# The last projection of a two-layer trunk: tiles 4 to 7 by Strassen's scheme

## The chip, the cores and the metric

The kernel runs on one core of a Trainium2 chip. The metric is the device time of one execution in microseconds. A core has five engines that run side by side, each with its own in-order queue of instructions: TensorE (PE; PEld is its loading of weights), VectorE (DVE), ScalarE (ACT), GpSimd (POOL) and SyncE (SP, which here only issues transfers; ScalarE's queue issues some as well). They meet through semaphores. TensorE writes to eight banks of PSUM, from which VectorE and ScalarE read.

## What is computed

Two layers, each with one mixer of three head groups, on 1024 tokens of 1024 values in float32:

```python
def hybrid_layer(x, c_act, positions, ...):
    mod = c_act @ w_mod + b_mod
    shift, scale, gate = jnp.split(mod[:, None, :], 3, axis=-1)
    h = rms_norm(x, pre_gain) * (1.0 + scale) + shift
    proj = h @ w_in
    ...   # a_out: windowed attention; r_out: retention; g_out: gated linear attention, each times its gate
    y = jnp.concatenate([a_out, r_out, g_out], axis=-1) @ w_out
    return x + gate * rms_norm(y, post_gain)
```

The change concerns `y = concat(...) @ w_out` and the line after it, in the second layer only, and there the second half of the tokens.

## The kernel before

**Tiles.** The 1024 tokens are eight tiles of 128 (`NT`), in four pairs (`NP_`); the 1024 inner values are eight slices of 128 (`KT`, index k). A float32 product is made from two parts of each operand in the faster matmul type fp32r: a high part (a rounded copy) and a low part (the rest). `PASSES` takes high x high, low x high and high x low, so that 128 tokens by 512 columns by all 1024 inner values are 3 x 8 = 24 matmuls into one PSUM bank (`accum`).

**Weights** lie in seven places of two arenas (`PLACES`), high and low part side by side. In the last layer, the output weights `o0` to `o3` (256 columns each) stand in places 3 to 6; places 0 and 1 hold the normalised input of tiles 4 to 7, and place 2 the last gate weights, all of them used for the last time by the gate products just ahead of the output projection. `unit(l, name)` gives a place; `both(x, y)` joins two slices of 256 columns into one operand of 512.

**The mixed tiles.** The output of the heads goes to DRAM as `mixS[t]`: for every tile the high and the low part, 8 slices of 128x128 each, transposed. Slices 4 to 7 (retention, linear attention) come from `head_norm_gate` through `store_mix`; slices 0 to 3 (attention) from `gate`, for four tiles at a time. The last `gate` stores end just after 903 us of the profile. `load_mix(l, t)` brings a tile back in two transfers of 512 KB into one of two `mx` buffers (tile 7, by `MIXP`, into an arena place that is free by then).

**The output stage.** For each tile, two calls of `y_half` (one for each 512 columns) run 24 matmuls each, then ScalarE squares the bank and sums (line 1247) and VectorE multiplies it by the gate (1248). `finish` works out the row's factor (lines 534, 528, and a power on GpSimd, 529), loads the residual `xs`, adds (1292) and stores to `out`. For the last layer's tiles 6 and 7 the first halves run before the second halves. The last half of tile 7 is `y_last`: two pieces of 256 columns, so that less is left to do behind the last matmul (lines 1257 to 1266).

**Order.** TensorE's instructions run in the order in which the program emits them. That order comes from a clock that the program keeps while it is built (`clk`): every matmul adds its cost, `flag(name, lat)` says when a result will be there (the latencies are in the table `L`), `await_flag` moves the clock on, and work that waits for something is a generator given to `job`, which `pump` continues when its time has come. The instructions of the other engines and of the transfer queues are put in order by the tile framework, by when their inputs and buffers are ready in its own model; on the chip each queue then runs strictly in that order. Buffers are rings by tag: `t2` (12 of 128x512), `t1` (8 of 128x256), `st` (11, used for raw weights), `smx` (6, used by the softmax), `va` (8), `kT0` and `kT1` (one each, keys), `mx` (2), and PSUM in `mm` (5 banks) and `aux` (3). `EN` gives the engine of each small operation.

Of the kernel before, what the change touches and what calls it, by code (L numbers as in the profile page):

```python
# [10 lines left out]
F32 = mybir.dt.float32  # L11
# [6 lines left out]
P = 128  # L18
# [71 lines left out]
def trunk(ctx: ExitStack, tc: tile.TileContext, ins, cst, out):  # L90
# [161 lines left out]
    xs = dr.tile([NT, P, D], F32, name="xs")  # L252
    mixS = dr.tile([NT, P, 2, KT, P], F32, name="mixS")
# [996 lines left out]
    def y_last(l, mixt, ss, yg):  # L1250
        s3 = small(3)
        for u in range(2):
            pm = mm()[:, 0:256]
            w = unit(l, f"o{2 + u}")
            accum(pm, lambda a, k: mixt[:, a, k, :], lambda b, k: w[:, b, k, 0:256])
            c = slice(256 * u, 256 * u + 256)
            A.activation(yg[:, c], pm, AF.Square, accum_out=s3[:, u:u + 1])
            if u == 0:
                V.tensor_tensor(s3[:, 2:3], ss[:, 0:1], s3[:, 0:1], ALU.add)
                V.tensor_scalar(s3[:, 2:3], s3[:, 2:3], 1.0 / D, EPS, ALU.mult, ALU.add)  # L1260
                V.tensor_tensor(yg[:, c], pm, modg[l][:, 512 + 256 * u:768 + 256 * u], ALU.mult)
        r = small(1)
        q = V.scalar_tensor_tensor(r, s3[:, 1:2], 1.0 / D, s3[:, 2:3], ALU.mult, ALU.add)
        G.tensor_tensor(r, r, mhalf[:, 0:1], ALU.pow)
        with tc.issue_after(q.ins):
            V.tensor_tensor(yg[:, c], pm, modg[l][:, 768:1024], ALU.mult)
        return r

    def load_mix(l, t):
# [6 lines left out]
        if l == DEPTH - 1 and t in MIXP:  # L1276
            n, o, _ = PLACES[TOK[l][t // 2]]
            o += t % 2 * 2 * KT * P
            mixt = arenas[n][:, o:o + 2 * KT * P].rearrange("p (a k n) -> p a k n", a=2, k=KT)
        else:  # L1280
            mixt = mix_tile()
# [4 lines left out]
    def finish(l, t, ss, yg, r=None):  # L1286
        r = rstd2(ss) if r is None else r
        xt = [t2(), t2()]
        for j in range(2):
            sl = slice(512 * j, 512 * j + 512)  # L1290
            dma("lx", xt[j], x_in[0, t * P:(t + 1) * P, sl] if l == 0 else xs[t, :, sl])
            V.scalar_tensor_tensor(xt[j], yg[j], r, xt[j], ALU.mult, ALU.add)  # L1292
            dma("sx", out[0, t * P:(t + 1) * P, sl] if l == DEPTH - 1 else xs[t, :, sl], xt[j])
# [19 lines left out]
    def layer(l):  # L1313
# [121 lines left out]
        def gate(g, hf, kk, pm):  # L1435
# [9 lines left out]
            V.scalar_tensor_tensor(ao, th, 0.5, ao, ALU.mult, ALU.mult)  # L1445
            mh, ml = t2(F32R), t2(F32R)
# [13 lines left out]
        for hf in range(2):  # L1460
# [8 lines left out]
            if not hf:  # L1469
                load(l, "o0")  # L1470
                load(l, "o1")
        mx[0] = load_mix(l, 0)
# [17 lines left out]
        for t in range(NT - 2, NT):  # L1490
            r = None
            if t == NT - 1:
                r = y_last(l, hold[t][0], hold[t][1], hold[t][2][1])
            else:
                y_half(l, t, 1, hold[t][0], hold[t][1], hold[t][2][1])
            job(finish(l, t, hold[t][1], hold[t][2], r))
# [67 lines left out]
```

## Time and profile before

| | us |
|---|---|
| median of 3 runs | 971.76 (971.18 to 973.42) |
| profiled execution, its own time | 971.16 |
| its span in the profile | 969.4 |
| TensorE busy | 951.3 (98%) |
| VectorE busy | 640.2 (66%) |
| ScalarE busy | 410.1 (42%) |
| GpSimd busy | 272.5 (28%) |
| granted TensorE clock, mean | 0.996 |

How to read the lines that follow. A row of the timeline has the start, the length (both us), the engine, the line of the program, the operation, output<-inputs by name, and, in brackets, how long the engine had been idle and what ended that. A row of a group has the line, engine, operation and shapes, the count, then the busy time in us and the mean of one in ns, then the idle time of the engine just before and what ended it. A row of the stage table has, for a stretch of time, the busy time and the number of instructions of PE, PEld, DVE, ACT and POOL, then the granted clock, the mean busy share of the sixteen transfer engines and the GB/s they moved. Much of the program goes through small helpers: line 161 is every matmul, 150 every transfer of `dma`, 145 every ScalarE copy. Matmuls are pipelined, so a row's single length is more than the time from one matmul to the next.

### The profile page before, as it was taken

The page shows a single profiled execution, that of the slowest core. Times are in us where ns is not written, and L with a number is a line of the kernel's source. Part 1 is how long each engine was busy: PE and PEld are TensorE (multiplying, and loading weights), DVE is VectorE, ACT ScalarE, POOL GpSimd, SP SyncE. Part 2 cuts the span into 40 slices and gives each one's busy share as a digit, 9 for nine tenths or more (in the row PEclk, how much of TensorE's full clock was granted, in tenths as well). Part 3 has the DMA queues.
Part 4 walks back from the last instruction along what each step waited for, and adds up shares of the span by engine and source line. Part 5 has one row for each costly group of instructions (what it writes and reads, how often), then busy time and mean ns, then how long its engine had stood idle before and what let it go on. Part 6 is the DMA issues. An engine that isn't in the chain of part 4 may idle for free.

```text
span 969.4 us, 18061 instructions
## 1 busy us (share of the span) xinstructions
PE 951.3 (98%) x6513; PEld 829.4 (86%) x6513; DVE 640.2 (66%) x1525; ACT 410.1 (42%) x1119; POOL 272.5 (28%) x323
## 2 busy tenths in 40 slices
PE   6999999999999999999999999999999999999997
PEld 1799999989998877878889999998999887777886
DVE  6886857777777777655586485686776577763332
ACT  2777312354422666622455531134652166761111
POOL 3243011533430344511242110144423034441000
PEclk9999999999999999999999999999999999999999
DMA  9943314624335355677455160253222333555871
GB/s 313 320 146 110 111 56 129 187 77 112 115 102 150 98 168 180 218 242 237 172 166 172 50 180 22 83 155 92 80 86 77 120 88 105 158 174 174 261 238 65
DMA packets 124293, 140.30 MB, mean 145 GB/s; under 512 B 12734, under 2 KB 95528, under 8 KB 124204
## 3 DMA queue, kind: packets, MB, share of 16 engines
q1 hardware_dynamic: 116204, 127.43, 42.9%
q10 hardware_dynamic: 8000, 11.72, 3.4%
q8 instruction: 51, 0.84, 0.4%
q14 instruction: 38, 0.31, 0.1%
HBM read 102.42 MB, written 34.60 MB: 141 GB/s over the span
## 4 chain that ended last, share of the span: by engine, by line
PE 86%; DMA 7%; DVE 3%; issue 2%; POOL 1%; ACT 0%; SPq 0%; DVEq 0%; ACTq 0%; POOLq 0%
PE mm L161 67%; PE aux L161 15%; PE aux L176 4%; DMA wm<-in_w_mod_dram 2%; DMA t<-in_x_dram 1%; DMA st<-in_w_in_dram 1%; DMA xk<-in_x_dram 1%; DMA t<-aoS 1%; DMA st<-in_w_mod_dram 1%; POOL sm L529 1%; DVE acc L367 0%; DVE t L1292 0%; POOL arena L491 0%; DVE t L624 0%; DMA c_ident<-cst_ident_dram 0%
## 5 line engine op out<-in xcount | busy, mean ns | idle before, releaser
L161 PE MATMUL mm<-arena,arena 128*128 128x256 f32 (+2 forms) x1896 | 303.0, 315 | 1.4 <-ACT arena L628 0.7
L161 PE MATMUL mm<-arena 128*128 128x256 f32 (+2 forms) x1824 | 294.7, 317 | 0.0
L161 PEld LDWEIGHTS mm<-arena,arena 128*128 128x128 f32 x1896 | 261.8, 188 | 24.6 <-ACT arena L628 1.2
L161 PEld LDWEIGHTS mm<-arena 128*128 128x128 f32 x1824 | 255.4, 191 | 22.0 <-issue 1.2
L161 PE MATMUL mm<-arena,mx 128*128 128x512 f32 (+1 forms) x744 | 168.7, 386 | 0.0
L161 PEld LDWEIGHTS mm<-arena,mx 128*128 128x128 f32 x744 | 135.6, 188 | 29.1 <-issue 1.5
L529 POOL TENSOR_TENSOR sm<-sm,mhalf 128x4 f32<-128x4 f32 (+1 forms) x60 | 51.8, 863 | 294.8 <-DVE sm L528 285.3
L491 POOL TENSOR_TENSOR arena<-st,arena 128x512 fp32r<-128x512 f32 x55 | 80.3, 1467 | 91.3 <-ACT arena L145 34.7
L145 ACT ACTIVATE t<-aux 128x512 f32<-128x512 f32 (+1 forms) x96 | 48.7, 521 | 106.4 <-PE aux L176 44.9
L943 POOL TENSOR_TENSOR smx<-smx,sm 128x512 f32<-128x512 f32 x32 | 36.2, 1131 | 114.8 <-DVE sm L942 111.4
L491 DVE TENSOR_TENSOR arena<-st,arena 128x512 fp32r<-128x512 f32 x65 | 62.3, 969 | 4.7 <-PE mm L161 2.6
L145 ACT ACTIVATE arena<-st 128x512 fp32r<-128x512 f32 x82 | 48.5, 626 | 29.0 <-PE mm L161 13.0
L1247 ACT ACTIVATE t<-mm 128x512 f32<-128x512 f32 x30 | 17.9, 597 | 92.2 <-PE mm L161 40.3
L939 ACT ACTIVATE smx<-smx,sm 128x129 f32<-128x129 f32 x128 | 50.0, 393 | 14.0 <-DVE sm L936 13.9
L1248 DVE TENSOR_TENSOR t<-mm,modg 128x512 f32<-128x512 f32 x30 | 20.6, 689 | 48.6 <-ACT t L1247 48.5
L367 DVE SCALAR_TENSOR_TENSOR acc<-st,c_act,acc 128x512 f32<-128x512 f32 x60 | 47.3, 788 | 7.5 <-DMA st<-in_w_mod_dram 6.8
L1292 DVE SCALAR_TENSOR_TENSOR t<-t,sm,t 128x512 f32<-128x512 f32 x32 | 25.9, 846 | 39.7 <-DMA t<-xs 20.8
L176 PE MATMUL aux<-c_ident,t 128*128 128x128 f32 x288 | 45.5, 278 | 2.9 <-DVE t L602 2.9
L176 PEld LDWEIGHTS aux<-c_ident,t 128*128 128x128 f32 x288 | 34.9, 144 | 7.3 <-DVE t L602 4.2
L934 DVE COPY_PREDICATED smx<-c_curmask,aux 128x256 f32<-128x256 int32 x64 | 25.5, 447 | 15.0 <-ACT smx L145 10.4
L990 ACT ACTIVATE t<-aux 128x256 f32<-128x256 f32 x32 | 12.2, 382 | 54.1 <-PE aux L161 26.8
L995 DVE TENSOR_TENSOR t<-aux,sm 128x256 f32<-128x256 f32 x32 | 13.6, 425 | 30.8 <-POOL sm L529 30.8
(214 smaller groups left out, 1300.9 us busy)
## 6 DMA issues: line engine op xcount, KB each, us to landing
st<-in_w_in_dram SPq DMA_DIRECT2D x96, 256.0 KB
st<-in_w_mod_dram SPq DMA_DIRECT2D x64, 256.0 KB
mx<-mixS SPq DMA_DIRECT2D x30, 512.0 KB
mixS<-t SPq DMA_DIRECT2D x64, 128.0 KB
st<-in_w_out_dram SPq DMA_DIRECT2D x32, 256.0 KB
mixS<-t SPq DMA_DIRECT2D x32, 256.0 KB
wm<-in_w_mod_dram SPq DMA_DIRECT2D x12, 512.0 KB
t<-in_x_dram SPq DMA_DIRECT2D x24, 256.0 KB
```

The source lines that it names most:

```text
L145: A.activation(dst, src, AF.Copy)
L161: T.matmul(dst, lhsT, rhs, start=start, stop=stop)
L176: T.transpose(dst, src, idn)
L367: V.scalar_tensor_tensor(acc, wt, c_act[:, k:k + 1], acc, ALU.mult, ALU.add)
L491: i = (G if first == 0 and kc in LOG else V if first == 0 else eng(f"wlo{kc}")).tensor_tensor(wt[:, 1, 2 * kc:2 * kc + 2, 0:256], st, f(hi ...
L529: after[2] = G.tensor_tensor(r, r, mhalf[:, :w], ALU.pow)
L934: V.copy_predicated(sv, curmask.unsqueeze(1).to_broadcast((P, 2, P)), pv[:, :, n // P - 1, :])
L939: A.activation(sm[:, h, :], sm[:, h, :], AF.Exp, bias=mx[:, h:h + 1], accum_out=sums[:, h:h + 1])
L943: eng("pn").tensor_tensor(sm[:, :, 0:128], sm[:, :, 0:128], rs.unsqueeze(2).to_broadcast((P, 4, P)), ALU.mult)
L1247: A.activation(yg, pm, AF.Square, accum_out=ss[:, nh:nh + 1])
L1248: V.tensor_tensor(yg, pm, modg[l][:, 512 * nh:512 * nh + 512], ALU.mult)
L1292: V.scalar_tensor_tensor(xt[j], yg[j], r, xt[j], ALU.mult, ALU.add)
```

## The change

In the second layer, tiles 0 to 3 are projected as before. Tiles 4 to 7 are taken in two pairs (p = 2 and 3). Of a pair, the two tiles, the two halves of the inner dimension (slices 0 to 3 and 4 to 7) and the two halves of the columns make 2x2 blocks A11 to A22 (tile, inner half) and B11 to B22 (inner half, column half). In place of eight block products, seven are made (Winograd's form of Strassen's scheme), each of 12 matmuls:

| m | A operand | B operand |
|---|---|---|
| 1 | A11 | B11 |
| 2 | A12 | B21 |
| 5 | A21 + A22 | B12 - B11 |
| 6 | A21 + A22 - A11 | B22 - B12 + B11 |
| 7 | A11 - A21 | B22 - B12 |
| 4 | A22 | B21 - (B22 - B12 + B11) |
| 3 | A12 - (A21 + A22 - A11) | B22 |

The four output blocks are then sums of products: 1+2; 1+6+7+4; 1+6+7+5; 1+6+5+3.

`load_sums` loads the 1024x1024 output weights a second time (sixteen pieces of 128x512), forms the B sums on VectorE and splits them into high and low part: blocks 5, 6, 7 into places 0, 1, 2, block 4 over the place of B12 after tile 3's product. The sums use the `smx` buffers and four `t2` buffers. For the A sums, the mixed tiles 4 to 7 are now also stored in full precision (`mixW`, by `head_norm_gate` and `gate`); `operands` loads four 256 KB halves of a pair, forms the four sums on VectorE and splits them. Unsummed blocks still come from `mixS`: the pair's first tile whole, of its second only slices 4 to 7, in eight pieces into `va` buffers. `outputs` lists the order of products, forms the output sums on VectorE (a ScalarE copy for product 1), squares and multiplies them from SBUF, and gives `finish` the tile. The last product (3 of pair 3, `tail`) is made in two pieces of 256 columns. In `finish`, the store of the last layer's output is now given out 1.5 us of the program's clock after the addition.

```diff
@@ head_norm_gate
         store_mix(t, kt0, pt[:, 0:256].rearrange("p (k q) -> p k q", k=2), 2)
+        if l == DEPTH - 1 and t >= 2 * NCL:
+            w = t1()
+            copy("mw", w, pt[:, 0:256])
+            dma("smw", mixW[t, :, kt0:kt0 + 2, :], w.rearrange("p (k q) -> p k q", k=2))
@@ gate
+            if l == DEPTH - 1 and hf * 4 + 3 >= 2 * NCL:
+                dma("smw", rows(mixW, hf, k), ao.rearrange("p (t q) -> p t q", t=4))
@@ load_sums (new)
+        for k in range(4):
+            raw = [gp.tile([P, 4, 129], F32, tag="smx", ...)[:, :, 0:P] for _ in range(3)]
+            hold.append(t2())
+            for r, (row, col) in zip(raw + [wide(hold[k])], ((0, 0), (0, 1), (1, 1), (1, 0))):
+                kt = 4 * row + k
+                dma("lwb", r, w_out[l, kt * P:(kt + 1) * P, 512 * col:512 * col + 512]...)
+            yield lat("bl2" if k else "bl1", l)
+            b11, b12, b22 = raw
+            if k > 1:
+                A.activation(b22, b22, AF.Copy, scale=gncol[:, l:l + 1])
+                A.activation(hold[k], hold[k], AF.Copy, scale=gncol[:, l:l + 1])
+            eng("ws5").tensor_tensor(b11, b12, b11, ALU.subtract)
+            eng("ws7").tensor_tensor(b12, b22, b12, ALU.subtract)
+            eng("ws6").tensor_tensor(b22, b22, b11, ALU.subtract)
+            eng("ws4").tensor_tensor(wide(hold[k]), wide(hold[k]), b22, ALU.subtract)
+            split("wl5", 5, k, b11)
+            split("wl7", 7, k, b12)
+            split("wl6", 6, k, b22)
...
+        yield (0.0, "plain")
+        for k in range(4):
+            hi, lo = weights(l, 4, 0, k), weights(l, 4, 1, k)
+            A.activation(hi, halves(hold[k]), AF.Copy)
+            eng("wl4").tensor_tensor(lo, halves(hold[k]), f(hi), ALU.subtract)
+            yield lat("bl4", l)
@@ operands (new), total
+            eng(f"os{m}").tensor_tensor(dst, x, y, op)
+            A.activation(hi, dst, AF.Copy)
+            eng(f"ol{m}").tensor_tensor(lo, dst, f(hi), ALU.subtract)
@@ outputs (new), rules
+            def first_():
+                A.activation(q, B[1], AF.Copy)
+            def c11():
+                V.tensor_tensor(y11, B[2], q, ALU.add)
+                square(y11, s0[:, 0:1])
+                eng("cg").tensor_tensor(y11, y11, gate[0], ALU.mult)
+            def sixth():
+                V.tensor_tensor(u2, B[6], q, ALU.add)
+            def seventh():
+                V.tensor_tensor(e, B[7], u2, ALU.add)
+            def c21_():
+                V.tensor_tensor(q, B[4], e, ALU.add)
+                square(q, s1[:, 0:1])
+                eng("cg").tensor_tensor(q, q, gate[0], ALU.mult)
+            def c22():
+                V.tensor_tensor(e, B[5], e, ALU.add)
+                V.tensor_tensor(u2, B[5], u2, ALU.add)
+                square(e, s1[:, 1:2])
+                eng("cg").tensor_tensor(e, e, gate[1], ALU.mult)
+                job(finish(l, 2 * p + 1, s1, [q, e]))
...
+            def tail():
+                for u in range(2):
+                    c = slice(256 * u, 256 * u + 256)
+                    b3 = mm()
+                    product(p, 3, b3, True, True, u)
+                    V.tensor_tensor(u2[:, c], b3[:, c], u2[:, c], ALU.add)
+                    i = square(u2[:, c], s0[:, 1 + u:2 + u])
+                    ...
@@ module level
-MIXP = (7,)
+FIN2 = 1
+NCL = 2
+MMP = (1, 2, 3, 4, 5, 6, 7)
+ORDER = [(2, "load"), (2, "half"), (2, 1), (2, 2), (3, "load"), (2, 5), (2, 6), (2, 7), (2, 4), (3, "half"), (2, 3), (3, 1), (3, 5), (3, 6), (3, 7), (3, 2), (3, 4), (3, "tail")]
```

More of the change, by code (lines that the diff above doesn't have):

```diff
@@ L1248, in y_half @@
         V.tensor_tensor(yg, pm, modg[l][:, 512 * nh:512 * nh + 512], ALU.mult)
[L1250 to L1267, printed above, removed]
@@ L1269, in load_mix, with block, weights, halves @@
-    def load_mix(l, t):
+    BLOCKS = {5: 0, 6: 1, 7: 2}
+    def block(m):
+        n, o, w = PLACES[BLOCKS[m]]
+        return arenas[n][:, o:o + 2 * KT * 256].rearrange("p (a k n) -> p a k n", a=2, k=4)
+    def weights(l, m, b, k):
+        if m in BLOCKS:
+            return block(m)[:, b, k]
+        u = 2 if m > 2 else 0
+        kt = k + (4 if m in (2, 3) else 0)
+        return both(unit(l, f"o{u}")[:, b, kt, 0:256], unit(l, f"o{u + 1}")[:, b, kt, 0:256])
+    def halves(ap):
+        return ap.rearrange("p (s n) -> p s n", s=2)
@@ L1270, in load_mix @@
+    def load_mix(l, t, half=False):
         if t < 2:
@@ L1275, in load_mix @@
             await_flag(("mix", l, t, kt0))
[L1276 to L1281, printed above, removed]
+        if half:
+            ts = [gp.tile([P, P], F32R, tag="va", name=nm("mh"), bufs=VDB) for _ in range(8)]
+            for i in range(8):
+                dma("lmix", f(ts[i]), mixS[t, :, i // 4, 4 + i % 4])
+            return ts
+        mixt = mix_tile()
         for a in range(2):
```

138 lines of the change are left out of this document (129 added, 9 removed).

## The prediction

> **What bounds the kernel now.** I read the page's engine rows first: is one engine the bound over the whole span, and at which clock?
>
> ```profile
> span 969.4 us, 18061 instructions
> PE 951.3 (98%) x6513; PEld 829.4 (86%) x6513; DVE 640.2 (66%) x1525; ACT 410.1 (42%) x1119; POOL 272.5 (28%) x323
> PEclk9999999999999999999999999999999999999999
> ```
>
> TensorE is busy for 98% at full clock, so work taken from it counts, if nothing then keeps it waiting. The change acts on the end of layer 1, so I next read its stretch of the chain that ended last (one line: start, us, what), and then the last microseconds of the timeline.
>
> ```profile
> 886.64 71.33 PE mm L161 x312
> ```
>
> ```profile
> 957.80 5.82 PE L161 MATMUL mm<-arena,arena 128*128 128x256 f32 x48
> ...
> 963.65 0.38 ACT L1257 ACTIVATE t<-mm 128x256 f32<-128x256 f32 x1 [2.29 <-DMA out_dram<-t]
> 963.93 0.19 ACT L1257 ACTIVATION_READ_ACCUMULATOR t<-mm 128x1 f32 x1
> 964.16 0.16 DVE L1263 SCALAR_TENSOR_TENSOR sm<-sm 128x1 f32<-128x1 f32 x1 [1.95 <-ACT t L1257]
> 964.24 0.42 DVE L1266 TENSOR_TENSOR t<-mm,modg 128x256 f32<-128x256 f32 x1
> 964.40 0.55 POOL L1264 TENSOR_TENSOR sm<-sm,mhalf 128x1 f32<-128x1 f32 x1 [4.10 <-DVE sm L1263]
> 964.98 1.42 DVE L1292 SCALAR_TENSOR_TENSOR t<-t,sm,t 128x512 f32<-128x512 f32 x2 [0.33 <-POOL sm L1264]
> ```
>
> From 886.64 on TensorE runs through without a break. The 312 matmuls are tiles 1 to 6 at 48 each and the first half of tile 7 (24): 71.33/312 = 0.2286 us for one 512 columns wide. The 48 of 256 columns that follow take 5.82/48 = 0.1213 us each. So tiles 4 to 7 begin at 886.64 + 3 x 48 x 0.2286 = 919.56 and their last matmul ends at 963.62. Behind it stand square, row factor, power and the last two multiply-adds (to 966.40), then the last transfer: 5.8 us to the span's end. Last, the stage table: what room have the engines that get the new work?
>
> ```profile
> core 0: us, PE busy (x) PEld busy (x) DVE busy (x) ACT busy (x) POOL busy (x), PEclk, DMA share, GB/s
> 860.00:880.00 20.00, 20.00 (x128) 15.31 (x127) 9.76 (x17) 9.56 (x31) 6.34 (x8) 1.00 0.59 185
> 880.00:900.00 20.00, 20.00 (x97) 15.80 (x96) 6.28 (x14) 2.64 (x9) 0.96 (x2) 1.00 0.55 180
> 900.00:920.00 20.00, 20.00 (x90) 16.32 (x89) 6.04 (x11) 2.09 (x7) 0.81 (x2) 1.00 0.91 292
> 920.00:940.00 20.00, 20.00 (x90) 16.56 (x89) 6.64 (x13) 2.62 (x8) 1.10 (x2) 1.00 0.76 257
> ```
>
> VectorE and ScalarE have two thirds free; the transfers have not, least of all between 900 and 920, just ahead of the tiles that are changed.
>
> **Part 1, the matmuls.** A pair had 2 tiles x 2 column halves x 2 halves of the inner dimension, eight blocks of 12 matmuls; now seven. Before, the two pairs took 963.62 - 919.56 = 44.06 us. After, 13 blocks of 12 at 0.2286 = 35.66 us and the last block in two halves, 24 at 0.1213 = 2.91 us: 38.57 us. Term: **-5.5 us**. The number of matmuls is fixed by the code, so that the change does not do this is no rival. By this clock pair 2 runs from 919.56 to 938.8, pair 3's sixth block ends at 955.2 and the last matmul at 958.1.
>
> **Part 2, the weight sums** (load_sums): sixteen loads of 256 KB; per k four sums and three low parts on VectorE, three high parts on ScalarE, and later the fourth block. The nearest rows, of the same shape:
>
> ```profile
> L1448 DVE TENSOR_TENSOR t<-t,t 128x512 fp32r<-128x512 f32 x4 | 3.1, 770 | 1.0 <-PE aux L161 0.9
> L1248 DVE TENSOR_TENSOR t<-mm,modg 128x512 f32<-128x512 f32 x15 | 10.3, 691 | 38.1 <-ACT t L1247 38.1
> L1292 DVE SCALAR_TENSOR_TENSOR t<-t,sm,t 128x512 f32<-128x512 f32 x16 | 11.3, 749 | 21.8 <-DMA t<-xs 20.8 <-POOL sm L529 0.7 <-POOL sm L1264 0.3
> L528 DVE TENSOR_SCALAR sm<-sm 128x1 f32<-128x1 f32 x7 | 1.1, 154 | 0.2
> L534 DVE TENSOR_TENSOR sm<-sm 128x1 f32<-128x1 f32 x7 | 1.1, 151 | 0.0
> L1247 ACT ACTIVATE t<-mm 128x512 f32<-128x512 f32 x15 | 9.0, 598 | 63.1 <-DVE t L1292 34.4 <-PE mm L161 28.7
> ```
>
> At 0.69 (the PSUM row; the row with both inputs in SBUF has 0.77) the 28 instructions ahead of the pairs are 19.3 us of VectorE, and 14 ScalarE copies at 0.60 are 8.4 us. The arena places that they write come free when the last gate product is done (about 870.5), and the first product with a summed block stands at 919.56 + 2 x 2.74 = 925.0. In those 54 us VectorE has about 19 us of old work by the table (half of the first row, two whole ones, a quarter of the last). Cost 0, covered by the plain tiles 0 to 3; if that cover is gone, the product of block 5 waits. The fourth block (four low parts, 2.8 us) is made after tile 3, since it overwrites weights that tile 3 reads, and is due at 933.3: 0. The four tiles that keep raw blocks leave eight of twelve t2 buffers for tiles 0 to 3, so their evictions may be late; ScalarE waited 34.4 us in five such waits (the L1247 row) and TensorE did not stall, with five banks to go on in. 0 again.
>
> **Part 3, the operand sums**: per pair four sums and four low parts on VectorE (8 x 0.69 = 5.5 us), four high parts on ScalarE (4 x 0.60 = 2.4 us). Pair 2's can begin once the last gates have stored their tiles, and are due one by one from 925.0 on. Counted with the output rules (11 VectorE passes of 512 a pair instead of 4), VectorE has between 919.56 and 955.2: rules 15 x 0.69 = 10.4, finishes of tiles 3 to 5 at 1.5 + 0.3 each = 5.4, tile 3's last product 0.7, pair 3's sums 5.5, the fourth block 2.8: 24.8 us of 35.6, and 30.3 (85%) if pair 2's sums also fall there. Under the bound: 0, with 0 to 3 us for the range.
>
> **Part 4, the transfers.** Added: 16 weight loads (4 MB), full-precision copies of the mixed tiles out (2 MB) and in (2 MB); 1 MB less of split tiles. SP gets some 48 more issues. What decides is the stretch ahead of 919.56:
>
> ```profile
> 904.00:906.00 2.00, 2.00 (x11) 1.65 (x10) 0.88 (x2) 0.65 (x2) 0.00 (x0) 1.00 1.07 354
> 936.00:938.00 2.00, 2.00 (x11) 1.65 (x10) 1.52 (x3) 0.69 (x2) 0.00 (x0) 1.00 1.01 397
> ```
>
> ```profile
> 907.88 2.76 SPq L150 DMA_DIRECT2D arena<-mixS  x2
> 910.69 0.90 SPq L150 DMA_DIRECT2D t<-xs  x2
> 911.69 1.16 SPq L150 DMA_DIRECT2D mx<-mixS  x2
> 917.46 1.41 DVE L1292 SCALAR_TENSOR_TENSOR t<-t,sm,t 128x512 f32<-128x512 f32 x2 [7.12 <-DMA t<-xs]
> ```
>
> Tile 4's split tile is issued at 911.69, when its buffer and the queue are free; the residual issued a microsecond before it was used only at 917.46, with VectorE waiting 7.12 us for it, so the queue was some 6 us deep. After the change tile 7's megabyte (907.88) is gone from this place, but both pairs' full-precision halves (2 MB), tile 5's halves (0.5 MB) and the last stores (0.5 MB) become ready just then, most of them before tile 4's buffer: 2 MB more. At 292/0.91 = 321 GB/s that is 6.2 us, of which the free 9% of the 20 us swallow 1.8: up to 4.4 us of lateness for the first product of pair 2. Ends 0 and 4.4; I take **+0.9**, near the low end, because that product needs only the first of tile 4's two transfers at first, and TensorE shows no wait of any size for a tile now. The block weights I put before 900, where these rows have room:
>
> ```profile
> 872.00:874.00 2.00, 2.00 (x11) 1.65 (x10) 1.97 (x4) 0.00 (x0) 1.46 (x2) 1.00 0.05 17
> 882.00:884.00 2.00, 2.00 (x11) 1.65 (x10) 0.00 (x0) 0.00 (x0) 0.00 (x0) 1.00 0.00 0
> 896.00:898.00 2.00, 2.00 (x10) 1.69 (x9) 0.63 (x2) 0.15 (x1) 0.00 (x0) 1.00 0.04 13
> ```
>
> The eight extra ScalarE copies and the stores of the mixed tiles before 870 lie beside a full TensorE: 0.
>
> **Part 5, the tail.** Square now follows an addition: 0.42 us (the 256-wide row L1266) and a handover, +0.45 us, on the path. Worse is what stands before it on VectorE. The sixth block of pair 3 ends at 955.2, and only 2.9 us of matmuls follow. In those fall two passes of the third output, three of the fourth (5 x 0.69 = 3.45), tile 7's row factor and first multiply-add (0.3 + 0.71), and the first half's addition, small sums and product (0.42 + 0.3 + 0.42): 5.6 us. If all of it goes first, the last addition comes 2.7 us late; if only the three additions and the first half's do (2.5 us), not at all. Middle 1.35. Tail +0.45 to +3.15; I take **+1.8**.
>
> Here the Trainium skill ("SBUF — State Buffer", section "Who interferes with whom") adds a price: a VectorE instruction with two SBUF inputs and a GpSimd instruction that reads SBUF exclude each other for the whole instruction. The trace agrees:
>
> ```profile
> 872.65 0.82 POOL L954 TENSOR_SCALAR_AFFINE_SELECT t<-t 128x512 f32<-128x512 f32 x1
> 873.00 1.00 DVE L1448 TENSOR_TENSOR t<-t,t 128x512 fp32r<-128x512 f32 x1
> ...
> 899.88 0.69 DVE L1448 TENSOR_TENSOR t<-t,t 128x512 fp32r<-128x512 f32 x1
> ```
>
> The same VectorE operation took 1.00 beside GpSimd and 0.69 alone. By that rule the last gate product, which now reads SBUF twice, could hold the power up by up to 0.42 us, and the sum would be that much higher.
>
> **The sum**: -5.5 + 0.9 + 1.8 = -2.8 us. The profiled execution took 971.16 us by its own time (span 969.4 and 1.8 around it); the median of the runs is 971.76, 0.6 above it. Taken from the median: **969.0 us**.
>
> **Rivals.** *A, as summed*: 967.9 to 969.7. *B, nearly the whole saving*: no wait for tile 4, VectorE's queue before the last addition short: 971.76 - 5.5 + 0.45 = 966.7. For it: TensorE never waited for a tile, and VectorE is at a third. Against it: the 5.6 us in a 2.9 us gap. *C, VectorE paces the pairs*: when pair 2's sums come only after 919.56, each product time of 2.74 us has to hold a sum and its low part (1.4) and a rule or two (0.7 to 2.1); three products late by about a microsecond each make 2.5 us, so about 971.5. For it: 85% in the table of part 3, and each low part waits for ScalarE in between. Against it: the stored tiles are there long before. *D, slower: the transfers before pair 2*. If the second half of the block weights (2 MB, buffers for it come free only as the first half is used up) also falls after 900, another 6.5 us at 321 GB/s go in front of tile 4; half of that with the 4.4 makes 7.7 in place of 0.9, so 975.8; the whole would be 979. It decides from a stall of 3.7 us (no gain) or 5.6 us (slower by 0.2%). For it: the share of 0.91 and the 7.12 us wait. Against it: the idle rows between 872 and 898.
>
> **How the numbers follow.** 0.2%, 1.9 us, is about what a measurement of this kernel tells from no change. A 0.40, B 0.18: faster 0.58. C and the small stalls of D 0.25: same. D proper 0.17: slower. The range reaches from under B (its 0.7 for what I did not find) to a D of some 5 us over A: 966.0 to 974.2. The likeliest case by itself: 967.9 to 969.7.
>
> **What would show it.** Right: the same matmul rate of 0.2286, no gap in TensorE's row from 887 to about 958, pair 2's first product at about 920, and from the last matmul to the end 7 to 8 us instead of 5.8. C shows as TensorE waits for operand tiles between 925 and 955; D as one wait for the mixed tile near 920 with the transfers' share at 1.0 from 900 on. Wrong would make me a shift before 886, where the order of TensorE's work is untouched, or a VectorE queue that delays the residual adds of tile 7 beyond the last tile.

## The result and the profile after

The kernel after the change takes **979.94 us** (median; 978.46 to 980.48) against 972.09 (971.18 to 973.42) before, which has one run more here than in the table above: ratio **1.0077 [1.006, 1.0095]**, slower by 7.85 us where 2.8 us less was forecast. The page's first rows for the kernel after:

```profile
span 976.8 us, 18169 instructions
PE 945.4 (97%) x6453; PEld 821.0 (84%) x6453; DVE 678.4 (69%) x1586; ACT 430.2 (44%) x1155; POOL 272.8 (28%) x323
```

TensorE is busy for 5.9 us less, and the span is 7.4 us longer: the work went, and more than its time came back as waiting. TensorE's rows in the timeline, from the end of attention on, show where:

```profile
887.79 16.77 PE L161 MATMUL mm<-arena,mx 128*128 128x512 f32 x72
905.44 5.75 PE L161 MATMUL mm<-arena,mx 128*128 128x512 f32 x24 [0.88 <-DVE t L1253]
912.34 12.24 PE L161 MATMUL mm<-arena,mx 128*128 128x512 f32 x52 [1.15 <-DMA mx<-mixS]
925.26 4.83 PE L161 MATMUL mm<-arena,mx 128*128 128x512 f32 x20 [0.68 <-DMA mx<-mixS]
932.64 8.60 PE L161 MATMUL mm<-arena,so 128*128 128x512 f32 x36 [2.55 <-DVE t L1253]
942.93 2.99 PE L161 MATMUL mm<-arena,mh 128*128 128x512 f32 x12 [1.69 <-DVE t L1384]
...
965.02 3.03 PE L161 MATMUL mm<-arena,so 128*128 128x256 f32 x24
```

Where one unbroken row stood before, there are five breaks; call them one to five. From start to start, less count x 0.2286, they are 1.19, 1.41, 1.03, 2.81 and 2.06: 8.5 us (the brackets give less, since a row's single length is more than a matmul's pace). The first, fourth and fifth wait for VectorE to empty a PSUM bank (lines 1253 and 1384), the second and third for a mixed tile. The stage table (PE, PEld, DVE, ACT, POOL, then clock, transfer share, GB/s):

```profile
880.00:900.00 20.00, 20.00 (x97) 15.79 (x96) 16.12 (x26) 10.79 (x20) 1.73 (x2) 1.00 1.00 295
900.00:920.00 20.00, 17.98 (x78) 14.06 (x77) 10.96 (x23) 2.76 (x10) 1.23 (x2) 1.00 0.97 298
```

Between 880 and 900 the transfers went from a share of 0.55 to 1.00, VectorE from 6.28 us to 16.12, ScalarE from 2.64 to 10.79. TensorE does not suffer there but behind it.

How long may a bank wait to be emptied? In the code the ring `mm`, which all output matmuls use, has three banks (`MMB = 3`), and `aux` has five; the description of the kernel before and the prediction have these two the wrong way round. So the bank of a half tile is needed again after two more halves: 2 x 24 x 0.2286 = 11.0 us. Before, the bank that was emptied latest was that of tile 3's first half, whose last matmul ends at about 914.1 by the pace of the prediction:

```profile
920.01 1.29 DVE L1248 TENSOR_TENSOR t<-mm,modg 128x512 f32<-128x512 f32 x2 [1.14 <-ACT t L1247]
```

The first of the two multiplications is over at 920.7, and the bank is needed again at 925.0: 4.3 us were left. In the kernel after, the last matmul of tile 1's first half ends at 893.28, and its bank is empty at 905.38, 12.1 us later and 1.1 too late. The timeline of the other engines shows how this first break comes about:

```profile
900.52 0.68 DVE L1280 TENSOR_TENSOR arena<-raw,arena 128x512 fp32r<-128x512 f32 x1
901.12 0.15 DVE L535 TENSOR_TENSOR sm<-sm 128x1 f32<-128x1 f32 x1
...
902.13 1.42 DVE L1485 SCALAR_TENSOR_TENSOR t<-t,sm,t 128x512 f32<-128x512 f32 x2 [0.67 <-POOL sm L530]
902.92 1.00 ACTq L150 DMA_DIRECT2D out_dram<-t  x2
903.97 0.60 ACT L1252 ACTIVATE t<-mm 128x512 f32<-128x512 f32 x1 [3.91 <-DVE t L1485]
904.69 0.69 DVE L1253 TENSOR_TENSOR t<-mm,modg 128x512 f32<-128x512 f32 x1
```

Read it backwards. TensorE's matmul at 905.44 needs the bank that line 1253 empties at 904.69, after ScalarE's square at 903.97. That square stands in ScalarE's queue behind the store of tile 0, which waits for tile 0's residual addition (902.13); this needs the row factor, whose first step (901.12) stands in VectorE's queue behind the last block sum and low part (900.52); and these had waited for the raw weights (ScalarE's line 1291 at 896.21, idle for 0.99 us before it). None of these engines is busy for much more than 16 of the 20 us, but the steps wait for one another in order, and the last of them is TensorE's.

The fourth and the fifth break, 4.9 of the 8.5 us, come about through the operand sums of part 3 (line 1324). VectorE's timeline:

```profile
928.88 0.69 DVE L1324 TENSOR_TENSOR st<-st,st 128x512 f32<-128x512 f32 x1 [2.29 <-DMA st<-mixW]
929.49 2.49 DVE L1306 TENSOR_TENSOR arena<-t,arena 128x512 fp32r<-128x512 f32 x4
931.90 0.68 DVE L1253 TENSOR_TENSOR t<-mm,modg 128x512 f32<-128x512 f32 x1
...
939.65 2.02 DVE L1324 TENSOR_TENSOR st<-st,st 128x512 f32<-128x512 f32 x3
941.59 0.69 DVE L1326 TENSOR_TENSOR so<-st,so 128x512 fp32r<-128x512 f32 x1
942.19 0.69 DVE L1384 TENSOR_TENSOR t<-mm,t 128x512 f32<-128x512 f32 x1
```

Pair 3's first sum (928.88) waits 2.29 us for its transfer, though TensorE needs it only at 951.20. Behind it in VectorE's queue, and behind the low parts of block 4 (929.49), stands the line that empties tile 3's last bank (931.90) for product 5. Pair 3's other three sums (939.65) stand ahead of line 1384, which empties the bank of product 6 for product 4. A product has 12 matmuls where a half tile has 24, so these banks are due sooner: tile 3's last after 5.5 us of matmuls, that of product 6 after 2.7, since product 5 holds the third until product 4 is done.

The span's 7.4 us are: -5.5 (matmuls), +8.5 (breaks), +2.9 (tail: 8.75 us from the last matmul to the end, before 5.8), and +1.2 that was there when the output projection began (871.98 against 870.76); with 0.3 of rounding. The 1.2 are put down to the run, which is not shown: over the kernels below that landmark lies between 870.3 and 874.2, on both sides of before's, and the differences are mostly there at 88 us already (the same matmuls begin at 87.80 in the kernel after and at 85.88 before).

### The profile page after: what moved, and what is told of

Read it like the earlier page. It is cut to its first block, busy times and chain, and to the rows that moved or that the text cites. A ratio compares the mean times of both kernels' runs of the same rounds, so it can differ in the third digit from the quotient of the medians.

```text
span 976.8 us, 18169 instructions
## 1 busy us (share of the span) xinstructions
PE 945.4 (97%) x6453; PEld 821.0 (84%) x6453; DVE 678.4 (69%) x1586; ACT 430.2 (44%) x1155; POOL 272.8 (28%) x323
## 5 line engine op out<-in xcount | busy, mean ns | idle before, releaser
L161 PE MATMUL mm<-arena,arena 128*128 128x256 f32 (+2 forms) x1824 | 291.9, 315 | 3.8 <-ACT arena L489 1.5
L161 PEld LDWEIGHTS mm<-arena,arena 128*128 128x128 f32 x1824 | 251.6, 188 | 26.3 <-ACT arena L629 2.3
L161 PE MATMUL mm<-arena,mx 128*128 128x512 f32 x624 | 147.9, 394 | 2.7 <-DMA mx<-mixS 1.8
L161 PEld LDWEIGHTS mm<-arena,mx 128*128 128x128 f32 x624 | 115.9, 188 | 30.3 <-DVE t L1253 2.8
L145 ACT ACTIVATE t<-aux 128x512 f32<-128x512 f32 (+1 forms) x104 | 51.7, 510 | 102.0 <-PE aux L176 36.8
L492 DVE TENSOR_TENSOR arena<-st,arena 128x512 fp32r<-128x512 f32 x65 | 60.3, 942 | 5.5 <-PE mm L161 2.8
L935 DVE COPY_PREDICATED smx<-c_curmask,aux 128x256 f32<-128x256 int32 x64 | 25.5, 447 | 17.3 <-ACT smx L145 12.1
L1252 ACT ACTIVATE t<-mm 128x512 f32<-128x512 f32 x24 | 14.3, 595 | 43.9 <-DVE t L1485 13.3
L145 ACT ACTIVATE t<-mm 128x256 f32<-128x256 f32 x40 | 14.9, 380 | 37.3 <-PE mm L161 21.5
```

The lines of the kernel that those rows point to most:

```text
L145: A.activation(dst, src, AF.Copy)
L161: T.matmul(dst, lhsT, rhs, start=start, stop=stop)
L492: i = (G if first == 0 and kc in LOG else V if first == 0 else eng(f"wlo{kc}")).tensor_tensor(wt[:, 1, 2 * kc:2 * kc + 2, 0:256], st, f(hi ...
L935: V.copy_predicated(sv, curmask.unsqueeze(1).to_broadcast((P, 2, P)), pv[:, :, n // P - 1, :])
L1252: A.activation(yg, pm, AF.Square, accum_out=ss[:, nh:nh + 1])
```

## The experiments

The time of the kernel before, beside which each of these stands, was between 970.98 and 971.74 us.

**What the blocks of the weights cost (part 2, forecast 0).** Three kernels leave out the loads, the sums, or both. In `load_sums`:

```diff
 no_block_loads
-                dma("lwb", r, w_out[l, ...])
+                G.memset(r, 0.01)
 no_block_math
-            eng("ws5")... eng("ws7")... eng("ws6")... eng("ws4")...; split(...) x3
+            for r in raw + [wide(hold[k])]:
+                V.tensor_copy(small(1), r[:, 0, 0:1])
 no_blocks: neither loads nor sums
```

> The second load of the output weights (sixteen transfers, 4 MB) is replaced by GpSimd fills of the same buffers with a constant; all sums, splits and products stay, so tiles 4 to 7 are made of wrong weights. Theory A (the 4 MB fill the transfer engines from 870 to 927, residuals come late, ScalarE's queue stands behind the stores that wait for them, and banks are emptied late): 972 to 974 us, the TensorE gaps between 900 and 943 nearly gone. Theory B (the sums' own work in VectorE's and ScalarE's queues delays the evictions): 977 to 980. Theory D (operand and output sums): 977 to 980.

> The sixteen transfers stay, but the sums and splits of the weight blocks are left out (32 VectorE and 20 ScalarE instructions of 512 columns); each loaded buffer is read by one VectorE copy of one column, and the products use what the places held before, so tiles 4 to 7 come from wrong weights. Theory A: 977 to 980. Theory B: 972 to 975. Theory D: 977 to 980.

> Neither the transfers nor the sums of the weight blocks: the whole of load_sums is gone, the products use what the places held before (wrong weights for tiles 4 to 7). What is left is operand sums, output sums, the added stores and the new tail. Theories A and B: 970 to 973 (5.5 us of matmuls saved, 3 us of tail lost, little else). Theory D: 976 or more.

Measured: without the loads 974.52 us, **1.0028 [1.0015, 1.004]**; without the sums 975.88, **1.0042 [1.0027, 1.0056]**; without both 970.03, **0.9978 [0.9966, 0.999]**. In us of before that is -4.8, -3.4 and -9.6 from the kernel after. Counted from the kernel with neither, the sums alone cost 4.9 us, the loads alone 6.2, both 9.6; by the intervals each of these is good to one or two us. So neither theory holds alone: the loads cost, and so do the sums. The kernel with neither also leaves out the four `t2` buffers that hold raw blocks; without the loads alone they stay. TensorE's timeline without either:

```profile
887.77 38.37 PE L161 MATMUL mm<-arena,mx 128*128 128x512 f32 x168
925.98 8.50 PE L161 MATMUL mm<-arena,so 128*128 128x512 f32 x36
935.21 3.01 PE L161 MATMUL mm<-arena,mh 128*128 128x512 f32 x12 [0.74 <-DVE t L1363]
```

No break up to product 4 of pair 2, although the tiles in full precision are still stored and loaded: without the block weights beside them, the mixed tiles' transfers, on which the prediction laid its +0.9, make TensorE wait for nothing. Product 4's bank comes 1.00 us late there from start to start, again behind pair 3's operand sums. Without the loads alone, 168 matmuls run through, the first four breaks shrink to one of 0.16, and what is left is the bank that product 4 needs:

```profile
925.18 8.77 PE L161 MATMUL mm<-arena,so 128*128 128x512 f32 x36 [0.16 <-DVE t L1253]
936.23 3.01 PE L161 MATMUL mm<-arena,mh 128*128 128x512 f32 x12 [2.28 <-DVE t L1384]
```

**ScalarE's queue.** The final stores go to SyncE's queue, so that no store stands ahead of an eviction.

```diff
-"sxl": "A"
+"sxl": "S"
```

> The stores of the last layer's output are issued by SP's queue instead of ScalarE's; nothing else. Theory C (it is the store issue in ScalarE's in-order queue, waiting for the residual addition, that holds up the evictions): 973 to 976. Theory A without C: 978 to 981, since SP's queue then waits in the same place and holds up loads.

Measured: 976.74 us, **1.0045 [1.0031, 1.006]**, 3.1 us back, with an interval that just meets that of the kernel after. The bank waits of line 1253 are gone, so the store in ScalarE's queue is a link of the chain, but not the only one there. The same square still waits for the addition in this kernel:

```profile
900.84 0.60 ACT L1252 ACTIVATE t<-mm 128x512 f32<-128x512 f32 x1 [2.92 <-DVE t L1485]
```

The two additions run from 899.99 to 901.41. The square begins when the first of them is over, where in the kernel after it began a microsecond after the first, behind both stores. The square writes into a `t2` buffer, and the additions give such buffers back; the last experiment bears on that. What is left is two waits for pair 2's tile, and they cost more than they show. TensorE's timeline and then the stage table over them:

```profile
887.39 33.01 PE L161 MATMUL mm<-arena,mx 128*128 128x512 f32 x144
922.91 1.15 PE L161 MATMUL mm<-arena,mx 128*128 128x512 f32 x4 [2.50 <-DMA mx<-mixS]
925.19 7.68 PE L161 MATMUL mm<-arena,mx 128*128 128x512 f32 x20 [1.13 <-DMA mx<-mixS]
```

```profile
924.00:926.00 2.00, 0.87 (x3) 0.72 (x3) 0.99 (x3) 0.00 (x0) 0.00 (x0) 0.61 0.89 268
926.00:928.00 2.00, 2.00 (x6) 1.51 (x6) 0.76 (x2) 0.63 (x1) 0.55 (x1) 0.50 0.86 292
928.00:930.00 2.00, 2.00 (x6) 1.56 (x5) 0.73 (x2) 0.60 (x1) 0.00 (x0) 0.50 1.00 345
930.00:932.00 2.00, 2.00 (x7) 1.55 (x6) 1.91 (x4) 0.63 (x1) 0.00 (x0) 0.68 0.83 311
```

The granted clock fell to half, and 20 matmuls took 7.68 us where the kernel after has 4.83 for 20.

**The tail.** VectorE's part of it in the timeline of the kernel after (the last matmuls are the row at 965.02 above, and the span ends at 976.8):

```profile
968.82 0.41 DVE L1412 TENSOR_TENSOR t<-mm,t 128x256 f32<-128x256 f32 x1
969.57 0.75 DVE L1485 SCALAR_TENSOR_TENSOR t<-t,sm,t 128x512 f32<-128x512 f32 x1 [0.33 <-POOL sm L530]
970.30 0.41 DVE L1417 TENSOR_TENSOR t<-t,modg 128x256 f32<-128x256 f32 x1
970.70 0.74 DVE L1485 SCALAR_TENSOR_TENSOR t<-t,sm,t 128x512 f32<-128x512 f32 x1
971.36 0.15 DVE L1419 SCALAR_TENSOR_TENSOR sm<-sm 128x1 f32<-128x1 f32 x1
```

The last matmul ends at 968.05, so the last addition is 0.8 us late; and the row factor's step (971.36) stands behind a product and tile 7's multiply-adds, of which the prediction counted one, and that ahead of the addition. One kernel gives those other outputs earlier (pair 3's products 2 and 4 are taken before 5); another, on top of it, hands the products with the gate to GpSimd.

```diff
 order_pair3
-(3, 1), (3, 5), (3, 6), (3, 7), (3, 2), (3, 4), (3, "tail")
+(3, 1), (3, 2), (3, 6), (3, 7), (3, 4), (3, 5), (3, "tail")
 tail_gate_pool: the same order, and
-"cg": "V"
+"cg": "G"
```

> Only the order of pair 3's products is changed: 1, 2, 6, 7, 4, 5, tail in place of 1, 5, 6, 7, 2, 4, tail, so that the third output's two VectorE passes stand one product earlier and only the fourth's three lie between the last whole block and the tail. If VectorE's queue is what lengthens the tail (8.75 us from the last matmul to the end against 5.8 before): 1 us or more faster than the change, 978 to 979 beside 980, and the stretch behind the last matmul under 8 us. If the tail is the chain itself (addition, square, power): no difference. The gaps before 943 stay.

> Pair 3 in the order 1, 2, 6, 7, 4, 5, tail, and the gate products of the output sums on GpSimd instead of VectorE. If VectorE's queue is what is left of the longer tail (7.7 us against 5.8 with the order alone): the tail shrinks by another microsecond, 975 to 977. If GpSimd's slower products (1.3 us against 0.7) and its queue take the place: 978 or more.

The order shortened the stretch behind the last matmul from 8.75 to 7.69 us (964.48 to 972.17). It is 7.4 to 7.8 in the three other kernels that have the order and the stores on SyncE's queue, and 9.3 against 10.7 in two with the stores on GpSimd's, all listed below; the time came to 977.26, **1.0057 [1.004, 1.0075]**, whose interval still meets that of the kernel after. With GpSimd the stretch grew to 9.2 and the ratio is **1.0076 [1.006, 1.0093]**, the second case of its text.

**One pair alone.** Tiles 6 and 7 by the scheme, 4 and 5 as before (`NCL = 3`), so half of the matmuls' saving, all of the blocks' work, and 96 matmuls (22 us) more until the first summed block. The mended one adds the new order and the stores on SyncE's queue.

> Only tiles 6 and 7 by the scheme (NCL = 3); tiles 4 and 5 plain. Half of the matmuls are saved (12, 2.7 us), the block weights are loaded and summed as before but due 22 us later, the operand sums are half. If the loss comes from the block weights' transfers and work whenever they fall: 977 to 980. If it comes from lateness ahead of the first pair: 972 to 975 (2.7 saved, 3 lost in the tail).

> Only tiles 6 and 7 by the scheme, the pair's products in the order 1, 2, 6, 7, 4, 5, tail, the output stores on SP's queue. One pair alone gave 1.0035 of before. If the order takes 1 us off the tail and the stores' move the one wait that is left ahead of tile 3 (1.2 us): 971 to 973, even with before. If SP's queue makes new waits: 974 to 976.

Measured: 974.59 us, **1.0035 [1.0022, 1.0048]**, and 975.71, **1.0037 [1.0023, 1.0051]**, each the second case of its text. One break is left in the first,

```profile
912.56 38.34 PE L161 MATMUL mm<-arena,mx 128*128 128x512 f32 x168 [1.16 <-DMA mx<-mixS]
```

yet nothing is saved: 2.7 us less of matmuls (half of the term) stand against 2.8 more behind them (8.6 instead of 5.8) and the break, 1.7 from start to start. That makes +1.7 or so of the +4.0 in the profile (+3.6 in the medians); the other 2.3 lie ahead of the output projection, 1.7 of them in the first 88 us, and why this kernel has them is not settled. In the second kernel the tail is 1.1 us shorter, but the breaks at the mixed tiles are 1.06 and 1.85, so the two edits together brought nothing here.

**The loads in other places.** First other buffers for the raw blocks; then these with the two edits above; then a quarter of each load's bytes, in the same places of the queue.

```diff
 raws_in_stage (and combined: this, "sxl": "S" and the order)
-            raw = [gp.tile([P, 4, 129], F32, tag="smx", ...)[:, :, 0:P] for _ in range(3)]
+            raw = [wide(stage()) for _ in range(3)]
 quarter_loads
-                dma("lwb", r, w_out[l, kt * P:(kt + 1) * P, 512 * col:512 * col + 512]...)
+                G.memset(r[:, 1:4], 0.01)
+                dma("lwb", r[:, 0:1], w_out[l, kt * P:(kt + 1) * P, 512 * col:512 * col + 128]...)
```

> The raw weight blocks go into the eleven 'st' buffers, which stand idle at that time, instead of the six 'smx' buffers that the softmax still holds, so that their transfers can start some 8 us earlier and need not wait for the sums. Theory A (when the 4 MB meet the stores, residuals and mixed tiles): 3 to 5 us faster than the change, 975 to 977. Theory B (the sums' work in the queues): at most 1 us faster.

> Raw blocks in 'st' buffers, output stores on SP's queue, and pair 3 in the order 1, 2, 6, 7, 4, 5, tail. If the three causes (transfers, ScalarE's queue, VectorE's queue in the tail) are separate: 3 to 5, 3 and 1 us add up, 971 to 973. If the first two are the same wait seen from two sides: 974 to 976.

> Each of the sixteen block loads brings only its first 128 columns (64 KB instead of 256 KB); GpSimd fills the rest with a constant, so the blocks are wrong. Entries in SP's queue, their waits for buffers, and all sums stay. Theory A (bytes): near the kernel with no block loads, 974 to 976. Theory E (places in SP's queue): 978 to 981.

Measured: **1.008 [1.006, 1.01]**, **1.0066 [1.0046, 1.0085]** and **1.0063 [1.0038, 1.0087]**. In the first only three loads came earlier (at 861 to 863), the others still from 877 on, so it did not make the test that it was meant to be. The ring `st` has five buffers in the code (`BST = 5`), not the eleven of the description and of the expectation, and so no room for a second group of three. The second is slower than either of its forecasts: the gains did not add. The last one's interval meets that of the kernel after and that without loads: it tells nothing of bytes against places.

The next pair loads straight into the arena places, so that no softmax buffer is waited for:

```diff
 arena_loads (and arena_loads_mended: this, "sxl": "S" and the order)
+        for i, m in enumerate((5, 7, 6)):
+            for k in (0, 2):
+                dma("lwb", f(block(m)[:, 1, k:k + 2]), mixS[2 * i + k // 2, :, :, 4:8]...)
-            raw = [gp.tile([P, 4, 129], F32, tag="smx", ...)[:, :, 0:P] for _ in range(3)]
+            r11, r12, r22 = [block(m)[:, 1, k] for m in (5, 7, 6)]
```

> Twelve of the sixteen loads of 256 KB become six of 512 KB that go straight into the arena places of blocks 5, 7 and 6, with no softmax buffer between; their data come from tiles 0 to 5 of the stored mixed tiles, slices 4 to 7 (rows of the same length), so the bytes are the same but the blocks are not the weights. The sums are made in place, as many and as long as before. If the loads cost by their places in SyncE's queue and by the buffers they wait for, they issue at about 871 to 875, the residuals of tile 0 are issued at about 888 again, the bank wait near 905 goes, and the ratio is that of the kernel without the loads, 1.002 to 1.004. If they cost by their bytes, the same 4 MB still fill the stretch from 870 to 905 and the ratio stays at 1.006 to 1.009.

> The same loads, and also pair 3's order 1, 2, 6, 7, 4, 5, 3 and the final stores on SyncE's queue. If places and in-order queues are the cause, the three gains add: 1.003 - 0.003 for the stores (half of it left, since the bank waits are gone already) - 0.002 for the order, so 0.998 to 1.001, the first version with all the work that is level with the kernel before. If bytes are the cause, about 1.004, as with the order and the stores alone.

Measured: 982.80 us, **1.0124 [1.0107, 1.014]**, and **1.0068 [1.0055, 1.0081]**; neither theory had that. The loads did go out at 868.91 to 873.9, but the work behind them now met attention instead. Timeline of the first, ScalarE, GpSimd and TensorE:

```profile
878.55 1.23 ACT L1300 ACTIVATE arena<-arena 128x512 fp32r<-128x512 f32 x2 [6.89 <-DVE arena L1295]
...
884.40 1.06 ACT L145 ACTIVATE t<-aux 128x512 f32<-128x512 f32 x2
885.04 7.83 POOL L955 TENSOR_SCALAR_AFFINE_SELECT t<-t 128x512 f32<-128x512 f32 x2 [11.70 <-ACT t L145]
889.91 0.85 PE L161 MATMUL aux<-t,vd 128*64 128x256 f32 x4 [4.24 <-POOL t L955]
892.92 1.12 PE L161 MATMUL aux<-t,vd 128*64 128x256 f32 x4 [1.30 <-POOL t L955]
893.97 39.84 PE L161 MATMUL mm<-arena,mx 128*128 128x512 f32 x168
```

Attention's copies (line 145) stood in ScalarE's queue behind the blocks' high parts (line 1300), which waited for the first sum, and the masks (line 955) for the copies. From 893.97 on TensorE runs 168 matmuls without a break, but it had by then lost some 6 us in which all else went on, so this does not tell bytes from places either. That question stays open.

**GpSimd's queue.** The block loads, the final stores, both (with the new order), and the low parts of blocks 5, 6 and 7 go to GpSimd.

```diff
 block_loads_on_pool:  "lwb": "S" -> "P"
 stores_on_pool:       "sxl": "A" -> "P"
 both_on_pool:         both, and the order of order_pair3
 low_parts_on_pool:    "wl7", "wl6", "wl5": "V" -> "G"
```

> The sixteen loads of raw weight blocks are issued by GpSimd's queue instead of SP's; same bytes, same sums. Theory E (the blocks' loads wait in SP's in-order queue for buffers that the sums give back, and the residuals and mixed tiles behind them start late): 974 to 977. Theory A (it is the bytes): 978 to 981.

> The last layer's output stores are issued by GpSimd's queue instead of ScalarE's, so that neither ScalarE's evictions nor SP's loads stand behind them. Theory C (ScalarE's queue stands behind the stores): 975 to 977, the bank waits (DVE line 1253 as releaser) gone and the waits for mixed tiles left. Without C: 978 to 981.

> Block loads and output stores both on GpSimd's queue, and pair 3 in the order 1, 2, 6, 7, 4, 5, tail. If C and E are separate waits and the bytes matter little: 969 to 972, at or under before. If the bytes are the main thing: 975 to 978.

> The twelve low parts of blocks 5, 6 and 7 go from VectorE (about 0.7 to 1.0 us each) to GpSimd; nothing else is changed. If the sums cost because they stand in VectorE's in-order queue ahead of the residual additions and row factors, twelve of 28 instructions taken away bring back some 40 to 60% of the 3.4 us that leaving all of them out brought: 1.0055 to 1.0065. If it is ScalarE's copies or the data's way through the softmax buffers, which GpSimd would hold longer, there is no gain or a loss: 1.0075 or more, with the loads of the second half of the blocks later than in the kernel after the change.

Measured: **1.0232 [1.0215, 1.0249]**, **1.0102 [1.0087, 1.0117]**, **1.0246 [1.0229, 1.0263]** and **1.0116 [1.01, 1.0131]**: none better, and all but the second, whose interval meets that of the kernel after, clearly worse. The waits of the first show where its time went:

```profile
PE aux L161 <- POOL t L955: 17.5, 2, 16.4
```

The loads are issued one by one, 3.5 to 6.3 us apart, with GpSimd idle for up to 5.5 us ahead of one; what it waits for there the trace does not name. Attention's mask stands in the queue behind them, and TensorE waits 16.4 us for it. With the stores there the bank waits of line 1253 went as expected, but TensorE waited 3.04 us for a mixed tile and the tail grew to 10.72. With the low parts on GpSimd there was no gain but a loss, the second case of its text; TensorE's wait for a mixed tile grew to 3.46 us (at 916.26), and attention's masks stood between the low parts there too.

**More buffers for the last evictions.** The residuals of the last layer take `st` buffers, which leaves the `t2` ring to the evictions.

```diff
-        xt = [t2(), t2()]
+        xt = [stage(), stage()] if l == DEPTH - 1 else [t2(), t2()]
```

> The last layer's residual tiles go into 'st' buffers instead of 't2', of which the raw blocks hold four. Theory F (it is the shortage of t2 buffers that makes residuals late): 975 to 977. If they are late for SP's queue or for the bytes: 978 to 981.

Measured: 982.38 us, **1.0115 [1.01, 1.013]**, worse. Yet the first break is gone: tile 1's first half is squared at 902.29, ahead of tile 0's additions (904.46), for which it waited in the kernel after. So the shortage of `t2` buffers was a condition of that break. The loss came elsewhere: the `st` ring with its five buffers also carries the operand halves, two operand sums waited 1.48 and 1.73 us for them just ahead of line 1384, and the wait for that line before product 4 grew from 1.69 to 4.91 us.

## Why the prediction was wrong

*What bounds the kernel, and part 1, held.* The matmuls keep their pace of 0.2286 (168 in 38.37 us), and without the blocks' work the stretch from the first output matmul (871.95 there) to the last is 88.39 us against 92.86: -4.5, which is -5.5 with the break of 1.00 before product 4. Without the blocks' work the kernel is 2.1 us faster, beside -2.8 forecast. That the two are so near is partly luck: the tail cost 1.1 more than its term, part 3 cost 1.0 instead of 0, and the +0.9 for the mixed tile was not needed.

*Part 2 failed, and decided the sign.* "Cost 0, covered by the plain tiles 0 to 3" weighed VectorE's busy time against a 54 us stretch. The work fits in that time (with 16 ScalarE copies in the code, not 14), and block 5 was not late for its product; but it stands in in-order queues among the evictions and residuals of the tiles that were meant to cover it. Measured: 9.6 us for loads and sums together. Part 2 did name what would happen, that the four `t2` buffers held by raw blocks could make the evictions late, and put it at 0 because TensorE had "five banks to go on in". It has three: 11.0 us for a half tile, of which 6.7 were in use before at the latest eviction, and 5.5 or 2.7 for a bank among the products. The other sentence that failed is "the block weights I put before 900, where these rows have room": the single rows shown there were empty, but the stage around them had a share of 0.55 already. Ten of the twelve loads into softmax buffers go out between 868 and 892, as those buffers come free, and filled it to 1.00.

*Part 3 failed in the same way.* "Under the bound: 0" again set a sum of busy times against a stretch. Two breaks, 4.9 us, passed through the operand sums in VectorE's queue; 1.00 of it is left when the blocks' work is gone, so the larger share comes of both together.

*Part 4* put a wait of +0.9 ahead of pair 2's first product; there were two waits for a mixed tile, for tile 3 and for the second transfer of tile 4, of 1.41 and 1.03 us, and without the blocks' work none. (The same 2 MB count as 6.2 us there and as 6.5 in rival D.) *Part 5* was mis-sized: +2.9 instead of +1.8, inside its ends of 0.45 and 3.15; the queue on VectorE was the reason named, and the order of products moved it by 1.06. Its row factor, not only its last addition, stood in that queue. The price of up to 0.42 for the power did not show: beside the last gate product it took 0.60 us (at 971.66), where it took 0.55 before.

*Rivals.* D had the sign, and with 975.8 (979 if whole) came nearest. Its premise did not come as it was put: the last raw block is there by 896.21, not after 900. But the transfers' share is 1.00 and 0.97 from 880 to 920, and tiles wait behind that. It failed in form too: not one wait for the mixed tile near 920, but a bank wait first, handed on by ScalarE's and VectorE's queues, from 904 on. C had VectorE pace the pairs. In the fourth and fifth break it does, but in another way: no row of TensorE waits for a summed operand, two wait for a bank that is emptied behind those sums. B is refuted with part 2. The chance of 0.17 for slower rested on "the idle rows between 872 and 898", which are the place that the added work filled.

What is shown by removal: the blocks' work as the cause, the store in ScalarE's queue and the shortage of `t2` buffers as links of the first break, the order of products as a third of the tail's loss. What is only read from the trace: VectorE's row factor behind the block sums, and the operand sums ahead of the fourth and fifth break. What stays open: bytes against places of the loads, and what more than three banks would have saved; no run gives the output products more. No version that does the whole computation beat the kernel before.

## What to carry to other kernels

Work that is put under a busy TensorE has to be placed in each in-order queue, not in an engine's idle share: ask which eviction stands behind it, what that eviction waits for already, and how long its PSUM bank may wait. Count the banks in the code, and turn them into time: three banks and 24 matmuls each gave 11.0 us here, and with 12 matmuls each 5.5. An old wait that costs nothing (34.4 us on ScalarE here) is not slack but a sign that the slack is in use. Price an added load at the stage where its buffer comes free, with the transfers' share of that stage after the addition.

## What the runs showed of the hardware

A break of TensorE can also cost clock. In the kernel with the stores on SyncE's queue, breaks of 2.50 and 1.13 us with four matmuls between were followed by a granted clock of 0.50, for about 6.8 us by the four rows of its stage table. Without the sums, one break of 2.03 us was followed by about 3.4 us of half clock (36 matmuls took 10.18 us there, and 8.60 in the kernel after). The Trainium skill ("TensorE: Matmul & The Clock Gate", section "What's actually happening") has half clock after an idle window of about 3.4 us; the traces agree on the half, and the lengths are about two and one such windows, but no single break was that long. In the profiled run of the kernel after, breaks of up to 2.55 did not trip it (mean clock 0.996, 978.46 us); its other executions have 0.992 to 0.994 and 979.88 to 980.48.

GpSimd can be held up by VectorE. With the loads in the arena two masks (line 955) took 4.82 and 3.05 us from 885.04 on (the profile's times on GpSimd are rough), while one took 0.63 at 872.71. VectorE's rows in the timeline of that kernel:

```profile
885.07 1.89 DVE L1301 TENSOR_TENSOR arena<-arena 128x512 fp32r<-128x512 f32 x3
886.87 1.29 DVE L1296 TENSOR_TENSOR arena<-arena 128x512 fp32r<-128x512 f32 x2
888.08 0.69 DVE L1297 TENSOR_TENSOR arena<-arena 128x512 fp32r<-128x512 f32 x1
888.68 0.69 DVE L1301 TENSOR_TENSOR arena<-arena 128x512 fp32r<-128x512 f32 x1
889.28 0.69 DVE L1253 TENSOR_TENSOR t<-mm,modg 128x512 f32<-128x512 f32 x1
```

The first four rows are operations with both inputs in SBUF, without a break; the last has one input in PSUM, and the first mask ends 0.6 us after it begins, at 889.86. Four more with both inputs in SBUF follow from 889.88 to 892.37, and the second mask ends 0.5 us behind them. The rule that the prediction weighed for the tail ("SBUF — State Buffer", section "Who interferes with whom", of the Trainium skill) has such an instruction contend with a GpSimd instruction that reads SBUF, over a lock on ports that they share; the trace agrees, and a row of such instructions kept a mask of 0.63 us waiting for several of them.
